# Sixteen operand tiles that each begin at another offset within 128 bytes

## The chip, the cores and the metric

The kernel runs on one core of a Trainium2 chip (trn2). The metric is the device time of one execution in microseconds (us). The core's engines are TensorE (PE in the profile; its weight loads, which run beside the matmuls, are PEld), VectorE (DVE), ScalarE (ACT), GpSimd (POOL) and SyncE (SP, here a queue for DMAs).

## The reference

One decoder block on x of 512 tokens x 1024 channels, float32. Two token mixers stand in parallel, a gated MLP in chunks (u, v_g) and a sparse attention whose keys an indexer selects (q, k, v, q_idx, k_idx). Their outputs are merged by sigmoid gates and projected; then comes a squared-ReLU MLP of 4096 channels.

```python
h = rmsnorm(x, norm1_g)
u, v_g, q, k, v, q_idx, k_idx, w_idx, gates = split_cols(h @ w_in, IN_SIZES)
y_a = sgu_mixer(gelu(u), gelu(v_g), w_s, b_s, sgu_ln_g, sgu_ln_b)
y_b = dsa_attention(rope(q), rope(k), v, rope(q_idx), rope(k_idx), w_idx)   # top 128 keys of a query
g = sigmoid(gates)                                                          # two gates
merged = g[0] * (y_a @ w_out_a) + g[1] * (y_b @ w_out_b)
x = x + merged @ w_o
h2 = rmsnorm(x, norm2_g)
x = x + square(relu(h2 @ w_ff_in)) @ w_ff_out
out = rmsnorm(x, norm_f_g)
```

## The kernel before

Activations are kept transposed, with channels on the 128 partitions and 512 tokens along them. A float32 product is made of three fp32r matmuls: each operand is split into a high part (ScalarE copies it to fp32r) and a low part (VectorE or POOL subtracts), and low x high, high x low and high x high are added in one PSUM bank. The input, scaled by the norm's weights, is 8 tiles `hTh[k]` (high) and 8 tiles `hTl[k]` (low) of 128 x 512, one pair for each 128 channels. After the attention the same 16 places hold `h2h[k]` and `h2l[k]`, the operand of the first MLP product.

`gemm` is the helper of most products. Its moving operand is the activation tile (512 columns), its stationary operand a 128 x 128 piece of a weight tile `wl` or `wh`; for each k it issues `wl[k]` with high (L146), `wh[k]` with low (L147) and `wh[k]` with high (L148). Each matmul has a weight load of its own. These products read the sixteen tiles as the moving operand:

- qi (index queries, 384 columns wide, 96 matmuls), k and q (96 each), ga and gb (the two gates, 192 each);
- f (the hidden layer of the MLP, `hidden`, 32 blocks of 24: 768).

Three more read them as the stationary operand, 128 tokens at a time: va at the start (values and the small index columns), and u and vg (`gmlp_in`, L409 to L411), where the weights `wh`, `wl` move.

Other products don't touch them: oa, ob (`yaT`, `ybs` moving), wo (`mT` moving), pp (`u` moving, `fp` stationary: the bulk of the second MLP product, in `products`), and the last part of that product (`f<-wh,fp`, L932 to L934: `wh`, `wl` moving, `fp` stationary).

The pools decide the addresses. In the built program every tile of `hTh`, `hTl`, `wh` and `wl` (pool G) begins at a multiple of 128 bytes in its partition. Pools E and F begin 96 bytes past a multiple of 128, and with them `mT`, `yaT`, `ybs`, `fp` and the tiles `u` that `products` uses. Pieces of a tile are 512 bytes or a multiple of it away from its beginning, so they stand at the same place within 128 bytes as the tile.

The order of the matmuls is that of a scheduler, which mixes neighbouring products; the generators `todo`, `fill` and `run` hand it the work.

Of the kernel before, what the change touches and what calls it, by code (L numbers as in the profile page):

```python
# [11 lines left out]
FR = mybir.dt.float32r  # L12
# [3 lines left out]
P = 128  # L16
S = 512
D = 1024
KD = D // P
# [14 lines left out]
def hybrid_block_kernel(ctx: ExitStack, tc: tile.TileContext, A: dict, out: bass.AP):  # L34
# [4 lines left out]
    G = ctx.enter_context(tc.tile_pool(name="G", bufs=1))  # L39
# [7 lines left out]
    def f32(ap):  # L47
        return ap.bitcast(F32)
# [125 lines left out]
        return get(0), get(1)  # L174


    hTh = [G.tile([P, S], FR, tag="hTh", bufs=KD, name=f"hTh{k}") for k in range(KD)]
    hTl = [G.tile([P, S], FR, tag="hTl", bufs=KD, name=f"hTl{k}") for k in range(KD)]
    VS = [E.tile([P, H, P], FR, tag="VS", bufs=NT, name=f"VS{j}") for j in range(NT)]
    R = E.tile([P, S], F32, name="R")  # L180
    rstd = G.tile([P, NT], F32, name="rstd")
# [43 lines left out]
    for t in raw2:  # L225
        t = f32(t.rearrange("p a b -> p (a b)"))
        raw += [t[:, i * NA:(i + 1) * NA] for i in range(3)]
    hl = []
    for k in range(KD):
# [5 lines left out]
        elif k < 6:  # L235
            t = E.tile([P, 13, P], FR, tag="pt", bufs=2, name=f"wa{k}").rearrange("p a b -> p (a b)")
# [486 lines left out]
    run(*[branch_b(m) for m in range(KD)])  # L723
    flush()

    h2h = [G.tile([P, S], FR, tag="hTh", bufs=KD, name=f"h2h{k}") for k in range(KD)]
    h2l = [G.tile([P, S], FR, tag="hTl", bufs=KD, name=f"h2l{k}") for k in range(KD)]
    x1T = []

    def proj_o(m):  # L730
# [357 lines left out]
```

## Time and profile before

| | us |
|---|---|
| median of 2 runs | 712.34 |
| lowest, highest | 711.14, 713.53 |
| profiled execution | 711.28 |
| its span, first to last instruction | 709.6 |
| TensorE busy in it | 693.9 |
| VectorE busy in it | 548.0 |

The length of a matmul in the profile runs from its start to its last result. The next one starts before that, so matmuls overlap in time, and the distance between two starts is what adds up.

### The profile page before, as it was taken

To read this page: it belongs to the slowest core of one execution; us is meant where nothing else is said; L and a number is where in the kernel's file an instruction comes from. 1 tells how busy PE (TensorE), PEld (TensorE's weight loads), DVE (VectorE), ACT (ScalarE), POOL (GpSimd) and SP (SyncE) were. 2 spreads that over 40 slices of the span, in tenths; PEclk is the share of its full clock that TensorE was granted. 3 is DMA by queue.
4 is the path that set the end of the run, shared out by engine and by line. 5 is a ranking of instruction groups with operands and counts; after the bars stand their busy time and mean duration, and the time that the engine had idled before them with its cause. 6 is when DMAs were issued, how large, how long until landed. Compare 5 with 4: busy or idle time off the path is not lost.

```text
span 709.6 us, 8958 instructions
## 1 busy us (share of the span) xinstructions
PE 693.9 (98%) x3232; PEld 575.1 (81%) x3232; DVE 548.0 (77%) x1015; ACT 329.7 (46%) x568; POOL 104.5 (15%) x61
## 2 busy tenths in 40 slices
PE   9999999899999899999999999999999999999996
PEld 8998888688887687778888888888888888888884
DVE  5588899976446857777442978979798997979995
ACT  5645633233244536564236765445352544535133
POOL 0053352444442242100000000000000000000001
PEclk9999999999999999999999999999999999999998
DMA  8735231234651454214443223142333214233023
GB/s 306 278 104 161 63 108 60 89 104 134 186 143 60 130 138 149 74 37 146 136 163 128 73 106 120 58 149 89 119 103 128 79 48 158 80 123 115 1 59 118
DMA packets 27356, 82.02 MB, mean 116 GB/s; under 512 B 4784, under 2 KB 6192, under 8 KB 25264
## 3 DMA queue, kind: packets, MB, share of 16 engines
q10 hardware_dynamic: 14688, 59.78, 26.0%
q1 hardware_dynamic: 12624, 21.67, 9.7%
q8 instruction: 25, 0.41, 0.2%
q14 instruction: 19, 0.16, 0.1%
HBM read 71.48 MB, written 2.10 MB: 104 GB/s over the span
## 4 chain that ended last, share of the span: by engine, by line
PE 59%; issue 0%; DVE 0%; ACT 0%; POOLq 0%; POOL 0%; ACTq 0%
PE f L148 8%; PE f L146 8%; PE f L147 8%; PE pp L882 6%; PE pp L884 6%; PE pp L883 6%; PE wo L146 2%; PE wo L147 2%; PE wo L148 2%; PE ob L146 1%; PE ob L147 1%; PE ob L148 1%; PE f L934 1%; PE f L933 1%; PE f L932 1%; PE pv L640 1%
## 5 line engine op out<-in xcount | busy, mean ns | idle before, releaser
L51 ACT ACTIVATE wh<-wr 128x1024 fp32r<-128x1024 f32 x88 | 92.9, 1057 | 127.2 <-PE f L148 40.4
L52 POOL TENSOR_TENSOR wl<-wr,wh 128x1024 fp32r<-128x1024 f32 x39 | 96.1, 2465 | 163.5 <-ACT wh L51 122.3
L146 PE MATMUL f<-h2h,wl 128*128 128x512 f32 x256 | 100.2, 391 | 0.0
L148 PE MATMUL f<-h2h,wh 128*128 128x512 f32 x256 | 100.0, 390 | 0.0
L147 PE MATMUL f<-h2l,wh 128*128 128x512 f32 x256 | 99.9, 390 | 0.0
L51 ACT ACTIVATE u<-w2r 128x512 fp32r<-128x512 f32 x98 | 59.1, 624 | 75.0 <-DVE w2r L810 25.4
L884 PE MATMUL pp<-u,fp 128*128 128x512 f32 x196 | 76.4, 390 | 0.0
L883 PE MATMUL pp<-u,fp 128*128 128x512 f32 x196 | 76.4, 390 | 0.0
L52 DVE TENSOR_TENSOR wl<-wr,wh 128x1024 fp32r<-128x1024 f32 x49 | 59.6, 1221 | 18.6 <-ACT wh L51 18.5
L882 PE MATMUL pp<-u,fp 128*128 128x512 f32 x196 | 72.1, 390 | 0.0
L895 DVE TENSOR_TENSOR P<-pp,P 128x512 f32<-128x512 f32 x84 | 54.4, 681 | 18.2 <-PE pp L884 18.0
L52 DVE TENSOR_TENSOR u<-w2r,u 128x512 fp32r<-128x512 f32 x98 | 64.4, 682 | 4.5 <-ACT u L51 4.5
L148 PEld LDWEIGHTS f<-h2h,wh 128*128 128x128 f32 x256 | 48.1, 188 | 10.1
L147 PEld LDWEIGHTS f<-h2l,wh 128*128 128x128 f32 x256 | 48.1, 188 | 10.0
L146 PEld LDWEIGHTS f<-h2h,wl 128*128 128x128 f32 x256 | 48.1, 188 | 9.9
L965 POOL TENSOR_TENSOR fss<-fss,mhalf 128x1 f32<-128x1 f32 x4 | 2.2, 547 | 317.7 <-DVE fss L964 317.7
L884 PEld LDWEIGHTS pp<-u,fp 128*128 128x128 f32 x196 | 36.8, 188 | 7.8
L882 PEld LDWEIGHTS pp<-u,fp 128*128 128x128 f32 x196 | 36.8, 188 | 7.8
L883 PEld LDWEIGHTS pp<-u,fp 128*128 128x128 f32 x196 | 36.8, 188 | 7.8
L51 ACT ACTIVATE fp<-fs 128x256 fp32r<-128x256 f32 (+1 forms) x28 | 17.6, 629 | 29.5 <-DVE fs L860 17.0
L838 DVE SCALAR_TENSOR_TENSOR fr<-f,R 128x512 f32<-128x512 f32 x32 | 21.8, 685 | 10.5 <-PE f L148 8.6
L146 PE MATMUL ga<-hTh,wl 128*128 128x512 f32 x64 | 25.1, 392 | 2.6 <-DVE mA L459 2.1
(251 smaller groups left out, 1563.5 us busy)
## 6 DMA issues: line engine op xcount, KB each, us to landing
wr<-in_f ACTq DMA_DIRECT2D x36, 512.0 KB, 3.5
w2r<-in_f2p ACTq DMA_DIRECT2D x14, 1024.0 KB, 4.9
wr<-in_wt ACTq DMA_DIRECT2D x26, 512.0 KB, 3.6
wr<-in_wuv ACTq DMA_DIRECT2D x8, 512.0 KB, 3.8
kq<-k_T SPq DMA_DIRECT2D x64, 64.0 KB, 2.2
wr<-in_wo ACTq DMA_DIRECT2D x8, 512.0 KB, 3.6
xT<-in_xT SPq DMA_DIRECT2D x8, 256.0 KB, 5.9
xn<-in_xn SPq DMA_DIRECT2D x2, 1024.0 KB, 9.1
```

Source lines behind the costliest of these rows:

```text
L51: ACT.activation(hi, src, AF.Copy)
L52: (eng or DVE).tensor_tensor(lo, src, f32(hi), op=ALU.subtract)
L146: PE.matmul(dst, wl[:, k], bh, start=(k == 0), stop=False)
L147: PE.matmul(dst, wh[:, k], bl, start=False, stop=False)
L148: PE.matmul(dst, wh[:, k], bh, start=False, stop=(k == K - 1))
L640: PE.matmul(b[:, s0 * P:], VS[j][:, h], rhs, start=(n == 0 and j == 0), stop=(n == 1 and j == NT - 1))
L838: DVE.scalar_tensor_tensor(r, b, 0.0, R2, op0=ALU.max, op1=ALU.mult)
L882: PE.matmul(b[j], fl, u[:, 0], start=(q == 0), stop=False)
L883: PE.matmul(b[j], fh, u[:, 1], start=False, stop=False)
L884: PE.matmul(b[j], fh, u[:, 0], start=False, stop=(q == 1))
L895: DVE.tensor_tensor(sums[name, j], b[j], sums[name, j], op=ALU.add)
L932: PE.matmul(b[j], fl[:, t], wh[:, k], start=(q == 0 and k == 0), stop=False)
```

## The change

Each of the sixteen tiles gets 32 more columns (128 bytes), and the 512 columns that are used begin at a column from a table: 0 to 30, another one for each tile. That is 0 to 120 bytes past the tile's beginning, which stays at a multiple of 128 bytes. The second use of the places, `h2h` and `h2l`, takes the same table. Nothing else is edited: the sequence of instructions on each of the five engines is the same in both built programs. The other tiles move up by 2048 bytes.

```diff
-    hTh = [G.tile([P, S], FR, tag="hTh", bufs=KD, name=f"hTh{k}") for k in range(KD)]
-    hTl = [G.tile([P, S], FR, tag="hTl", bufs=KD, name=f"hTl{k}") for k in range(KD)]
+
+    AT = dict(hTh=(0, 1, 2, 4, 8, 12, 16, 24), hTl=(26, 30, 3, 6, 10, 14, 20, 28))
+
+    def operand(tag, k, name):
+        t = G.tile([P, S + 32], FR, tag=tag, bufs=KD, name=f"{name}{k}")
+        return t[:, AT[tag][k]:AT[tag][k] + S]
+
+    hTh = [operand("hTh", k, "hTh") for k in range(KD)]
+    hTl = [operand("hTl", k, "hTl") for k in range(KD)]
...
-    h2h = [G.tile([P, S], FR, tag="hTh", bufs=KD, name=f"h2h{k}") for k in range(KD)]
-    h2l = [G.tile([P, S], FR, tag="hTl", bufs=KD, name=f"h2l{k}") for k in range(KD)]
+    h2h = [operand("hTh", k, "h2h") for k in range(KD)]
+    h2l = [operand("hTl", k, "h2l") for k in range(KD)]
```

## Rows read from the trace of the kernel before

**Rows 1.** The page: its head, TensorE's busy time with its share of the span and its instructions, and the clock granted to TensorE in 40 equal slices of the span (tenths, 9 is 90% or more).

```profile
span 709.6 us, 8958 instructions
...
PE 693.9 (98%) x3232; PEld 575.1 (81%) x3232; DVE 548.0 (77%) x1015; ACT 329.7 (46%) x568; POOL 104.5 (15%) x61
...
PEclk9999999999999999999999999999999999999998
```

**Rows 2.** Groups of TensorE's matmuls by line, tiles and shape: out<-in, count | busy us, mean ns of one | idle us before them.

```profile
L146 PE MATMUL f<-h2h,wl 128*128 128x512 f32 x256 | 100.2, 391 | 0.0
L148 PE MATMUL f<-h2h,wh 128*128 128x512 f32 x256 | 100.0, 390 | 0.0
L147 PE MATMUL f<-h2l,wh 128*128 128x512 f32 x256 | 99.9, 390 | 0.0
L884 PE MATMUL pp<-u,fp 128*128 128x512 f32 x196 | 76.4, 390 | 0.0
...
L147 PE MATMUL gb<-hTl,wh 128*128 128x512 f32 x64 | 25.3, 395 | 0.0
L147 PE MATMUL wo<-mT,wh 128*128 128x512 f32 x64 | 25.1, 396 | 0.0
...
L148 PE MATMUL ga<-hTh,wh 128*128 128x512 f32 x64 | 24.9, 389 | 0.0
...
L148 PE MATMUL oa<-yaTh,wh 128*128 128x512 f32 x32 | 12.7, 396 | 0.0
...
L934 PE MATMUL f<-wh,fp 128*128 128x512 f32 x32 | 12.6, 395 | 0.0
...
L148 PE MATMUL ob<-ybsh,wh 128*128 128x512 f32 x32 | 12.5, 395 | 0.0
...
L410 PE MATMUL u<-wl,hTh 128*128 128x512 f32 x32 | 12.4, 389 | 0.0
```

**Rows 3.** The timeline of TensorE in the middle of the f matmuls: start us, length us, engine, line. The first and the last of eleven matmuls that follow each other, and a weight load after the second of them (426 us).

```profile
425.75 0.39 PE L148 MATMUL f<-h2h,wh 128*128 128x512 f32 x1
425.97 0.39 PE L146 MATMUL f<-h2h,wl 128*128 128x512 f32 x1
...
428.01 0.39 PE L146 MATMUL f<-h2h,wl 128*128 128x512 f32 x1
...
425.98 0.19 PEld L147 LDWEIGHTS f<-h2l,wh 128*128 128x128 f32 x1
```

**Rows 4.** The same in the middle of the wo matmuls, the first and the last of eleven that follow each other.

```profile
339.82 0.40 PE L148 MATMUL wo<-mT,wh 128*128 128x512 f32 x1
...
342.15 0.40 PE L146 MATMUL wo<-mT,wl 128*128 128x512 f32 x1
```

**Rows 5.** Stretches of the span (us from its start): their length, then for PE, PEld, DVE, ACT and POOL the busy us (and instructions), the granted clock, the DMA share and GB/s. In this order: the f matmuls, the wo matmuls, and the gates ga beside VectorE's top-k work.

```profile
424.00:444.00 20.00, 20.00 (x90) 16.55 (x89) 16.35 (x27) 11.44 (x20) 0.00 (x0) 1.00 0.43 141
330.00:360.00 30.00, 30.00 (x130) 24.16 (x129) 15.48 (x18) 10.05 (x12) 0.00 (x0) 1.00 0.41 126
...
122.00:134.00 12.00, 9.36 (x41) 7.14 (x40) 12.00 (x23) 3.26 (x5) 4.94 (x2) 1.00 0.26 87
```

**Rows 6.** The timeline of TensorE among the qi matmuls, 384 columns wide: the first and the last of eleven that follow each other.

```profile
37.12 0.33 PE L147 MATMUL qi<-hTl,wh 128*128 128x384 f32 x1
...
38.85 0.33 PE L148 MATMUL qi<-hTh,wh 128*128 128x384 f32 x1
```

**Rows 7.** Instructions that read hTl, by product: count, then shortest/median/longest length in ns, start of the first and of the last in us, shape. The last row is from the same view of hTh.

```profile
L147 PE MATMUL ga<-hTl,wh x64: 389/389/398, 102.8 to 148.8; 128*128 128x512 f32 x64
...
L147 PE MATMUL gb<-hTl,wh x64: 387/389/478, 198.6 to 295.0; 128*128 128x512 f32 x64
...
L147 PE MATMUL qi<-hTl,wh x32: 334/334/346, 31.4 to 50.0; 128*128 128x384 f32 x32
...
L409 PE MATMUL vg<-wh,hTl x32: 387/396/397, 50.3 to 80.1; 128*128 128x512 f32 x32
...
L147 PE MATMUL k<-hTl,wh x32: 387/389/398, 149.5 to 228.1; 128*128 128x512 f32 x32
...
L147 PE MATMUL q<-hTl,wh x32: 389/389/477, 163.2 to 247.7; 128*128 128x512 f32 x32
...
L410 PE MATMUL vg<-wl,hTh x32: 389/393/398, 50.5 to 80.4; 128*128 128x512 f32 x32
```

**Rows 8.** The timeline of TensorE from 110 to 140 us, the two matmuls before which it sat idle: [idle us <-what ended it].

```profile
125.06 0.50 PE L146 MATMUL ga<-hTh,wl 128*128 128x512 f32 x1 [0.56 <-POOL wl L52]
...
132.87 0.47 PE L146 MATMUL ga<-hTh,wl 128*128 128x512 f32 x1 [2.08 <-DVE mA L459]
```

**Rows 9.** Operations of VectorE and ScalarE that write the sixteen tiles, as groups by shape (columns as in rows 2).

```profile
L739 DVE SCALAR_TENSOR_TENSOR h2l<-x1T,g,h2h 128x512 fp32r<-128x512 f32 x8 | 6.0, 747 | 1.6 <-ACT h2h L738 1.6
...
L284 ACT ACTIVATE hTh<-xT,g 128x512 fp32r<-128x512 f32 x8 | 5.7, 718 | 3.4 <-DMA xT<-in_xT 1.9 <-DMA g<-in_g 1.4
...
L738 ACT ACTIVATE h2h<-x1T,g 128x512 fp32r<-128x512 f32 x8 | 5.7, 714 | 6.6 <-DVE x1T L737 6.6
...
L286 DVE SCALAR_TENSOR_TENSOR hTl<-xT,g,hTh 128x512 fp32r<-128x512 f32 x7 | 5.3, 751 | 6.2 <-ACT hTh L284 6.2
```

**Rows 10.** The eight warm-up matmuls at the start: count, shortest/median/longest length in ns.

```profile
L281 PE MATMUL va<-wah x8: 628/628/793, 1.5 to 4.7; 128*128 128x512 f32 x8
```

## Prediction

> **What bounds the kernel now.** I read the page's busy shares first: TensorE is busy 693.9 of 709.6 us, at the full clock in nearly every slice [rows 1]. The next engine, VectorE, is at 77%. So the question is how long one matmul takes, and second where TensorE waits and could swallow a loss.
>
> The groups by shape give the length of one matmul [rows 2]. All of those I use are 128x512 fp32r, each with a weight load of its own, and still they fall into two families. The hidden products f, the gates ga, the u projection and the products pp have 389 to 391 ns. oa, wo, ob and the last products (`f<-wh,fp`) have 395 to 396 ns. Lengths overlap, because matmuls are pipelined; what counts is the distance between two starts. Among the f matmuls ten distances are 428.01 - 425.75 = 2.26 us, 226 ns each [rows 3]; among wo 342.15 - 339.82 = 2.33 us, 233 ns each [rows 4]. So the difference of the lengths, 6 to 7 ns, is also the difference in pace, at the same shape and the same clock of 1.00 in both windows [rows 5].
>
> What sets the families apart? I lay the built program's addresses beside the rows. Each time the weight load of the next matmul runs inside the current one (a load starts at 425.98 for 0.19 us, just after the matmul of 425.97) [rows 3]. Compare where the moving operand of the running matmul starts, within 128 bytes, with where the weights being loaded start. f, ga, u: both at 0. pp: both at 96. oa, wo, ob: moving 96, weights 0. Last products: moving 0, weights 96. Equal starts go with 389 to 391, unequal with 395 to 396, whichever of the two stands at 96. That pool E against pool G would explain it as well is a rival below.
>
> How much of a matmul is such meeting? The 384 wide qi matmuls, also with equal starts, follow each other at (38.85 - 37.12)/10 = 173 ns [rows 6]. From 384 to 512 columns the pace grows by 53 to 54 ns, 0.42 ns a column; 512 columns alone would be 212 to 216 ns, so the 227 hold 11 to 15 ns beyond columns, and the 233 hold 17 to 21. I take this excess as the price of the two reads meeting; that is an inference from the rows, not something that they show.
>
> **The change, part by part.** No instruction is added, removed or moved: the sequences of all five engines are the same in both built programs, so there is no new wait and no queue is moved past. SBUF grows by 16 x 128 = 2048 bytes a partition and the rest of the tiles move by multiples of 128, so oa, wo, ob, pp and the last products keep their pair of starts: 0. What changes is the start of hTh, hTl, h2h, h2l: 4 times the table's number, 0 to 120 bytes past a multiple of 128.
>
> Of the 24 matmuls of one projection (8 steps of k; high twice, low once) only the two with tile 0 of the high part keep equal starts: 22 of 24 become unequal. Price of one that becomes unequal: the step between the families, 6.5 ns (396 - 389.5). It is one step for one distance (96 bytes, or 32 the other way), and fifteen other distances are coming; the rows bound it from 0 (a distance that meets as little as equal starts) to 9 ns (the longest ga matmul that is not waiting, 398 against 389 [rows 7]). I take 6.5, since both unequal groups of the trace agree on it. Term by term:
>
> - Hidden products f: 768 x 22/24 = 704 at 6.5 ns = 4.6 us. They run with TensorE full and VectorE at 16.35 of 20 us [rows 5], so all of it is on the path.
> - Gates ga and the u projection: from 81 to about 130 us TensorE is ahead of VectorE. It waits 0.56 and 2.08 us there, for POOL and for VectorE's ga evacuation behind its top-k work [rows 8], and VectorE is full (12.00 of 12 us) while TensorE has 9.36 [rows 5]. u (88 x 6.5 = 0.6 us) and the ga before 132.9 us (some 110 x 6.5 = 0.7 us) fit into this 2.6 us: 0. Without that cover they would cost 1.3 us. The ga after it, from 133 to 149 us at 227 ns some 72, of which 66 unequal: 0.4 us.
> - gb, k, q: 384 matmuls, 352 unequal. They are mixed with attention work; the medians are still 389 [rows 7], the means 395 for gb [rows 2]. Part of the price is already paid by such neighbours, part falls into softmax waits: 5 ns, 1.8 us.
> - vg: medians 396 and 393 already [rows 7]: 88 at 1 ns, 0.1 us. qi, 384 wide, median 334: 88 at 4 ns, 0.35 us.
> - va at the start (192 matmuls, hT as weights): its moving operands mostly start at 96 against 0 now, so one unequal distance is replaced by another: 0, with 1.2 us either way as bound.
> - ScalarE and VectorE write and read these tiles in 32 operations of 714 to 751 ns [rows 9]; an element per lane and step is what they do at any start that the trace shows, and they are spread over stages where TensorE is full: 0.
>
> Sum: 4.6 + 0.4 + 1.8 + 0.1 + 0.35 = 7.2 us. The profiled execution took 711.28 us (span 709.6); 711.3 + 7.2 = 718.5. The median of the runs, 712.34, lies 1.06 above that execution: **719.5 us**, 1.0% slower. With 2 ns in place of 6.5 it is 714.5, with 9 ns 722.3: the forecast's own range is 714.5 to 722.5.
>
> **The rivals.**
>
> *No change.* The two families could be due to the pool (E against G: far apart in SBUF) or to who wrote the tile, not to the start within 128 bytes; the rows cannot separate these, as every E tile starts at 96. pp speaks against it a little: both its operands are in the late pool and it has 390 [rows 2], so it isn't the pool alone, but a pair of pools would still do. Or small distances count like 0. Then 712 us, 709.5 to 714.5.
> [...]
>
> *Slower by more than 2%: reads that straddle.* Every moving operand of the trace starts at a multiple of 32 bytes. Now 10 of 24 matmuls (k = 1, 2 of the high tiles, six of the low tiles) start off a multiple of 16, and 3 of 24 off a multiple of 8. If such a read fetches two pieces for each piece before, these alone get slower. At half pace, 227 ns more (the only rows with a much slower 128x512 are the eight warm-up matmuls at the very start, 628 against 389 ns long [rows 10]), 3 of 24 of 1344 matmuls are 168 x 0.227 = 38 us: 758 us; 10 of 24 would be 127 us. It decides from 14.2 - 7.2 = 7 us over 560 matmuls, 13 ns each; there the time is 727. For it: no row excludes it. Against it: 512 neighbouring elements need not be fetched anew for each.
> [...]
>
> *Faster.* Equal starts may be the bad meeting, and 96 a worse one, while other distances avoid it. If all of the excess of 12 ns went for the 704 + 66 + 352 + 88 = 1210 matmuls on the path, 14.5 us go: 698 us. A third of that, the likelier size since the distances are mixed: 707. Against it: the two distances known are both worse than 0, and 387 is the shortest length in the gb and k rows, 2 ns under their median [rows 7].
>
> **How the numbers follow.** Forecast 0.52, no change 0.24, straddling reads 0.14, faster 0.10. The likeliest gives 719.5. From 709 to 730: below lie some 0.07 of the faster case, above some 0.12 of straddling, so 0.81 is inside. 2% (about what a measurement of this kernel can tell from no change) is 14.2 us: 698.1 and 726.6. Faster by over 2%: 0.03, which takes all of the excess; slower: the straddling rival and a tail of the forecast with over 12 ns a matmul, 0.17; within: 0.80.
>
> **What the profile after would show.** Right: f goes from 390 to about 396 ns and u from 389 to 396, while pp (390), oa and wo (396) stay, and the counts, the waits and the clock stay. The mean may split by line: the two lines with hTh against the one with hTl. Wrong: f at 390 (pool, not start); f bimodal with some far above 400 (straddling), to be seen in the largest of the length of `f<-h2l,wh` against the other two lines; f below 387 (faster). If f has its 396 and the time hasn't grown, the path is elsewhere than I think. If pp or wo move as well, the start isn't what acts but the place in SBUF.

## Result and profile after

The changed kernel takes 720.09 us (median of 2 runs, 719.27 to 720.90) against 712.34: ratio 1.0105, 95% interval 1.0072 to 1.0137. That is slower by more than the runs scatter and by less than 2%. The profiled execution took 719.27 us.

The head of the page after answers to [rows 1]: the same instructions and the same clock, and TensorE is busy 7.1 us longer in a span that is 7.9 us longer.

```profile
span 717.5 us, 8958 instructions
...
PE 701.0 (98%) x3232; PEld 576.4 (80%) x3232; DVE 551.8 (77%) x1015; ACT 330.3 (46%) x568; POOL 104.1 (15%) x61
...
PEclk9999999999999999999999999999999999999998
```

The groups of TensorE after (count | busy us, mean ns | idle us before) answer to [rows 2].

```profile
L148 PE MATMUL f<-h2h,wh 128*128 128x512 f32 x256 | 101.5, 397 | 0.0
L146 PE MATMUL f<-h2h,wl 128*128 128x512 f32 x256 | 101.3, 396 | 0.0
L147 PE MATMUL f<-h2l,wh 128*128 128x512 f32 x256 | 101.0, 394 | 0.0
L891 PE MATMUL pp<-u,fp 128*128 128x512 f32 x196 | 76.4, 390 | 0.0
...
L147 PE MATMUL gb<-hTl,wh 128*128 128x512 f32 x64 | 25.5, 398 | 0.0
L148 PE MATMUL ga<-hTh,wh 128*128 128x512 f32 x64 | 25.4, 397 | 0.0
L147 PE MATMUL wo<-mT,wh 128*128 128x512 f32 x64 | 25.1, 395 | 0.0
...
L148 PE MATMUL oa<-yaTh,wh 128*128 128x512 f32 x32 | 12.7, 396 | 0.0
...
L417 PE MATMUL u<-wl,hTh 128*128 128x512 f32 x32 | 12.6, 395 | 0.0
```

f, u and ga have joined the longer family; pp, wo and oa stand where they were. The pace went with the length: in the timeline after, twelve distances between f matmuls are 433.41 - 430.62 = 2.79 us, 232.5 ns each, against 226 in [rows 3].

```profile
430.62 0.40 PE L148 MATMUL f<-h2h,wh 128*128 128x512 f32 x1
...
433.41 0.40 PE L148 MATMUL f<-h2h,wh 128*128 128x512 f32 x1
```

Where the time went is read from the start of each product's first matmul, before and after: from row to row the lag grows. The view by tile (count, shortest/median/longest ns, first to last start) answers to [rows 7]; the third row is from the same view of h2l, whose row before ran from 367.6 to 679.5 us.

```profile
L147 PE MATMUL ga<-hTl,wh x64: 388/395/403, 103.9 to 150.3; 128*128 128x512 f32 x64
L147 PE MATMUL gb<-hTl,wh x64: 387/394/477, 200.5 to 299.2; 128*128 128x512 f32 x64
...
L147 PE MATMUL f<-h2l,wh x256: 388/395/480, 371.8 to 687.5; 128*128 128x512 f32 x128
```

ga begins 103.9 - 102.8 = 1.1 us later, gb 1.9, the last gb 4.2, f 4.2, the last f 8.0. So 3.8 us are lost inside f, about half of the whole, 2.3 while gb runs among the attention's matmuls, and 1.1 before ga.

### The profile page after: what moved, and what is told of

Read it like the earlier page. It is cut to its first block, busy times and chain, and to the rows that moved or that the text cites. A ratio compares the mean times of both kernels' runs of the same rounds, so it can differ in the third digit from the quotient of the medians.

```text
span 717.5 us, 8958 instructions
## 1 busy us (share of the span) xinstructions
PE 701.0 (98%) x3232; PEld 576.4 (80%) x3232; DVE 551.8 (77%) x1015; ACT 330.3 (46%) x568; POOL 104.1 (15%) x61
## 4 chain that ended last, share of the span: by engine, by line
PE 59%; issue 0%; DVE 0%; ACT 0%; POOLq 0%; POOL 0%; ACTq 0%
PE f L148 8%; PE f L146 8%; PE f L147 8%; PE pp L891 6%; PE pp L890 6%; PE pp L889 6%; PE wo L146 2%; PE wo L147 2%; PE wo L148 2%; PE ob L146 1%; PE ob L147 1%; PE ob L148 1%; PE f L941 1%; PE f L939 1%; PE f L940 1%; PE pv L647 1%
## 5 line engine op out<-in xcount | busy, mean ns | idle before, releaser
L148 PE MATMUL f<-h2h,wh 128*128 128x512 f32 x256 | 101.5, 397 | 0.0
L148 PEld LDWEIGHTS f<-h2h,wh 128*128 128x128 f32 x256 | 48.1, 188 | 11.1
```

The lines of the kernel that those rows point to most:

```text
L148: PE.matmul(dst, wh[:, k], bh, start=False, stop=(k == K - 1))
```

## The experiments

The theory on record: what counts is where, within 128 bytes, the moving operand of a matmul starts against where the weights start that are loaded beside it. Rivals: the place in SBUF; the pool (E against G); that neighbouring matmuls differ in their distance (the "mixture" below); reads that straddle, from starts off 16 bytes. "Distance" below is the start of the moving operand less that of the weights. The runs of the kernel before beside these had medians of 711.6 to 711.9 us (712.8, one run, beside the scan by 4 bytes and the last experiment).

**Longer tiles alone.** The changed kernel with all offsets zero.

```diff
-    AT = dict(hTh=(0, 1, 2, 4, 8, 12, 16, 24), hTl=(26, 30, 3, 6, 10, 14, 20, 28))
+    AT = dict(hTh=(0,) * KD, hTl=(0,) * KD)
```

> The sixteen tiles are 128 bytes longer as in the change, all begin at column 0. Theory (the distance within 128 bytes between the start of the moving operand and of the weights that load beside it): all distances are 0 again, so f<-h2h,wh has a mean of 390 ns, as before (397 with the change), and the time is that of the kernel before, 712 us, ratio 1.000. Rival (the place in SBUF: tiles moved by up to 2048 bytes): f at 396, ratio 1.010.

Measured: 717.62 us, 1.0074 (1.0056 to 1.0092). Its groups:

```profile
L147 PE MATMUL f<-h2l,wh 128*128 128x512 f32 x256 | 101.0, 395 | 0.0
L148 PE MATMUL f<-h2h,wh 128*128 128x512 f32 x256 | 101.0, 394 | 0.0
L146 PE MATMUL f<-h2h,wl 128*128 128x512 f32 x256 | 100.9, 394 | 0.0
```

Every tile starts at the same place within 128 bytes as before, and still f has 394 to 395: the theory modulo 128 falls. A tile is now 2176 bytes long, 8.5 times 256, so every second one starts 128 away modulo 256. The theory put on record next was modulo 512 (a tile is 4.25 times that); the scan by 16 bytes below makes 256 of it. The rival of this run, the place in SBUF as such, forecast 396 and isn't refuted by it; the control below does that.

**All offsets 96 bytes.** `AT` is 24 for every tile.

> All sixteen tiles begin at column 24, 96 bytes past a multiple of 128, so the distance to the weights is one and the same in all of f, ga, gb, k, q. Theory: the distance of 96 that oa and wo have, so f and ga get their 396 ns; f 768 x 6.5 ns = 5.0, ga after VectorE's wait 0.5, gb, k, q 1.9, the rest 0.5, together 7.9 us: 720, ratio 1.011. Rival pool (oa and wo are slow as their moving operand is in the late pool, not for its start): f stays at 390, ratio 1.000. Rival mixture (it costs that neighbouring matmuls differ in their distance, not the distance itself): f stays at 390, ratio 1.000.

Measured: 719.02 us, 1.0092 (1.0073 to 1.0111), f at 395 to 398. As the theory said, but this doesn't support it: the long tiles, which the run above found guilty, are in here too.

**Pools E and F moved by 32 bytes** in the kernel before, so that the moving operands of oa, wo and ob, and the weights of the last products, start at distance 0 from their partners. The sixteen tiles are left alone.

```diff
+    G.tile([P, 8], F32, name="pad")
```

> The kernel before, with 32 bytes of padding at the end of the first pool, so that the pools E and F begin at a multiple of 128 too and every operand of the kernel has distance 0. Theory: oa, ob, wo and the last products (480 matmuls) go from 396 to 390 ns, 480 x 6.5 = 3.1 us: 709.2, ratio 0.9956. Rival pool: they stay at 396, ratio 1.000.

Measured: 709.11 us, 0.9947 (0.9932 to 0.9963).

```profile
L147 PE MATMUL wo<-mT,wh 128*128 128x512 f32 x64 | 24.7, 389 | 0.0
...
L148 PE MATMUL oa<-yaTh,wh 128*128 128x512 f32 x32 | 12.4, 389 | 0.0
...
L932 PE MATMUL f<-wh,fp 128*128 128x512 f32 x32 | 12.4, 389 | 0.0
```

All three groups fell from 395 or 396 to 389. They stay in their pools, so the pool as a cause falls. This one line makes the fastest kernel of the study, ahead of both the kernel before and the one after. Its gain is larger than the medians say: in its profile the granted clock was 0.80 from 130 to 136 us (1.00 before), and k's first matmul starts 2.2 us later than before; yet the span is 2.0 us shorter, so some 4 us are gained behind that.

**The same pools moved by 160 bytes**: distance 0 modulo 128, but 128 modulo 256.

```diff
+    G.tile([P, 40], F32, name="pad")
```

> As e3, but with 160 bytes of padding: the later pools begin at a multiple of 128 which is 256 past a multiple of 512, where the first pool's tiles are 128 past one. Theory (modulo 512): oa and wo stay at 394 to 396 ns, ratio 0.999 to 1.001. Rival (modulo 128): 390 as in e3, ratio 0.995.

Measured: 711.48 us, 1.000 (0.9989 to 1.0011).

```profile
L147 PE MATMUL wo<-mT,wh 128*128 128x512 f32 x64 | 25.1, 395 | 0.0
...
L148 PE MATMUL oa<-yaTh,wh 128*128 128x512 f32 x32 | 12.6, 395 | 0.0
```

With 32 bytes of padding 389, with 160 again 395. Between these two runs nothing differs but the 128 bytes: modulo 128 is refuted without the long tiles (256 and 512 both stand).

**Offsets without longer tiles.** Each eight tiles become pieces of one tile, laid in the order of their offsets so that none overlaps; first with all offsets zero as a control, then with the table.

```diff
+    def operands(tag, name):
+        t = G.tile([P, KD * S + 128], FR, tag=tag, bufs=1, name=name)
+        out = [None] * KD
+        for p, k in enumerate(sorted(range(KD), key=lambda k: AT[tag][k])):
+            out[k] = t[:, p * S + AT[tag][k]:(p + 1) * S + AT[tag][k]]
+        return out
...
```

> The eight high tiles are pieces of one tile of 8 x 2048 + 512 bytes, the eight low ones of another, each piece at a multiple of 2048 from the beginning: every start is 128 past a multiple of 512, as in the kernel before, and all other tiles keep their place within 512 bytes. No instruction moves. Theory now (the distance modulo 512 bytes between the start of the moving operand and that of the weights loaded beside it; a distance of 0 gives 227 ns from start to start, others 229 to 236): f at 390 ns, 712 us, ratio 1.000. Rival (the place in SBUF as such: the other tiles stand 1024 bytes higher): f above 393, 715 or more.

> The same, with the table's offsets of the change (0 to 120 bytes) in pieces that otherwise begin at 128 past a multiple of 512: the offsets without the longer tiles. Theory (distance modulo 512): nearly all distances are unequal to 0, f at 395 to 397 ns, 718 to 720 us, ratio 1.009 to 1.011; the offsets and the longer tiles cost much the same each, and not their sum together. Rival (the longer tiles alone do it, and offsets under 128 add the third that is missing, 717.6 to 720.1): f at 391 to 392, 714 to 715.

Measured: the control 713.20 us, 1.0015 (1.0006 to 1.0024), f at 390 to 391; with the table 716.86 us, 1.0076 (1.0061 to 1.0091), under the 718 to 720 expected, f at 394 to 395. In the control f has its length of before, though the other tiles stand 1024 bytes higher: the place in SBUF falls. The 2.1 us by which its profile's span is longer don't come from distances. k's first matmul already starts 2.1 us later than before, and f's last 2.2; 1.6 of it came while ga ran, behind TensorE's wait of 2.1 us for VectorE. There the granted clock (the value before the DMA share; the control, then before) was 0.71 on the mean of 5 us, against 1.00 before:

```profile
135.00:140.00 5.00, 5.00 (x17) 4.02 (x16) 5.00 (x16) 1.58 (x2) 2.88 (x2) 0.71 0.31 75
135.00:140.00 5.00, 5.00 (x23) 4.13 (x22) 5.00 (x15) 1.58 (x2) 2.87 (x2) 1.00 0.36 105
```

So the offsets alone cost about as much as the longer tiles alone, and both together (1.0105) less than the sum: f has 394 to 395 ns with either and 394 to 397 with both, so a matmul that was off already didn't get off twice.

**Which distances.** Only the weights of the f matmuls are moved here, 16t bytes further in block t (24 matmuls, t from 0 to 31), with the high and the low half in one tile; h2h and h2l stay. In the next run, the same with 4t bytes.

```diff
-            h = G.tile([P, 1024], FR, tag="wh", bufs=3, name=f"wh{n}")
-            l = G.tile([P, 1024], FR, tag="wl", bufs=3, name=f"wl{n}")
+            w = G.tile([P, 2 * 1024 + 128], FR, tag="wh", bufs=3, name=f"w{n}")
+            o = at_w.get(n, 0)
+            h, l = w[:, o:o + 1024], w[:, o + 1024:o + 2048]
...
+    at_w.update({len(wsrc) + m: 4 * m for m in range(4 * NG)})
...
```

> The kernel before, with high and low weights of a step in one tile; the 32 blocks of f have their weights begin 16 t bytes further, block t = 0 to 31, all else as before. One distance for all of a block. Theory (modulo 512): block 0 at 227 ns from start to start, the others at 229 to 236, blocks 8, 16 and 24 (128, 256, 384) among them, mean about 232. Rival (modulo 128): blocks 8, 16 and 24 at 227 like block 0. Rival mixture (what costs is that the distance changes between neighbouring matmuls): all blocks at 227.

Measured: 714.60 us (one run). The starts of the first matmuls of blocks 15, 16 and 17, and of 23, 24 and 25:

```profile
512.55 0.40 PE L148 MATMUL f<-h2h,w 128*128 128x512 f32 x1
...
518.01 0.39 PE L148 MATMUL f<-h2h,w 128*128 128x512 f32 x1
...
523.45 0.39 PE L148 MATMUL f<-h2h,w 128*128 128x512 f32 x1
...
595.07 0.39 PE L148 MATMUL f<-h2h,w 128*128 128x512 f32 x1
...
600.67 0.40 PE L148 MATMUL f<-h2h,w 128*128 128x512 f32 x1
...
606.27 0.39 PE L148 MATMUL f<-h2h,w 128*128 128x512 f32 x1
```

Block 16 (weights 256 bytes further) takes 523.45 - 518.01 = 5.44 us, 226.7 ns a matmul: as if not moved. Block 24 (384 further, 128 modulo 256) takes 5.60, 233.3 ns. The expectation (modulo 512) missed with block 16, and the mixture falls with block 24, whose matmuls all have one distance. Over the run, blocks t and t + 16 have nearly the same pace, leaving out the first three and their partners, as other matmuls come between the first: in this scan of 0 to 496 bytes the pace repeats after 256. At distances 0 and 16 it is about 227, at 64 and 80 229 to 230, at the rest 232 to 234. Block 17, at distance 240, kept 227, but block 1, at the same distance, did so only at its start:

```profile
374.97 0.39 PE L148 MATMUL f<-h2h,w 128*128 128x512 f32 x1
...
376.10 0.40 PE L150 MATMUL f<-h2h,w 128*128 128x512 f32 x1
...
379.94 0.40 PE L150 MATMUL f<-h2h,w 128*128 128x512 f32 x1
...
382.04 0.40 PE L150 MATMUL f<-h2h,w 128*128 128x512 f32 x1
```

The first five distances between starts make 1.13 us, 226 ns each; then transposes (`xn`) come between, and the last nine make 2.10 us, 233 ns each. So at one distance this run has both paces, and what ran before them differs.

> As e7, but in steps of 4 bytes: the weights of block t of f begin 4 t bytes further, t = 0 to 31, so distances of 0 to -124 bytes, three of four off a multiple of 16. Theory (the distance modulo 256 bytes, as e7 showed it: 0, 16 and 240 at 227 ns from start to start, 64 and 80 at 229 to 230, the others at 232 to 234): blocks 0 and 4 (distance 0 and 240) at 227, blocks off a multiple of 16 between 226 and 236 like those on one. Rival straddling (a read that starts off 16 or 8 bytes takes longer): blocks off 16 bytes stand above all of e7's, over 236, the odd ones most.

Measured: 715.37 us (one run). The first and the last matmul of blocks 21 (84 bytes) and 25 (100 bytes), 23 distances each:

```profile
565.42 0.39 PE L148 MATMUL f<-h2h,w 128*128 128x512 f32 x1
...
570.82 0.39 PE L150 MATMUL f<-h2h,w 128*128 128x512 f32 x1
...
607.01 0.39 PE L148 MATMUL f<-h2h,w 128*128 128x512 f32 x1
...
612.30 0.39 PE L150 MATMUL f<-h2h,w 128*128 128x512 f32 x1
```

Block 21 is the slowest, 5.40/23 = 235 ns; block 25 has 5.29/23 = 230. Weights that start off 16, 8 or 4 bytes lie between 227 and 235, where the multiples of 16 lie too. So no load that starts off 16 bytes stands above the 236 that the rival asked for; the straddling rival of the prediction was about the moving operand, and there the kernel after decides: `f<-h2l`, with six of eight steps off a multiple of 16, has 394 ns, the least of the three f lines. So the straddling rival falls. The expectation of 227 at distance 240 missed again (block 4: 233), while block 30, at 136, has 227.

**A scan that told little.** As the scan by 4, but with each half in a tile of its own, longer by 128 bytes.

> The kernel before, where the weight tiles of the 32 blocks of the hidden products begin at another column each: block t at column t, so at 4 t bytes, high and low alike. Within a block all 24 matmuls have one distance, -4 t bytes. Theory: the distance between two starts of f differs by block, 227 ns for block 0, about 233 for block 24 (weights at 96, moving at 0, as in the last products), the others between 224 and 238; the mean over the blocks near the 233 of f in the changed kernel. Rival mixture: each block at 227, since nothing changes within a block. Rival straddling: the 24 blocks whose column is no multiple of 4 stand apart from the 8 others, above all the odd columns.

Measured: 718.16 us (one run), f at 395 on all three lines. The longer tiles move every second buffer by 128 bytes, so that in each block either the high or the low weights are 128 bytes off the distance they were given: inconclusive, and the reason for the one-tile form above.

**Which of the two weights.** Only the low half of the f weights is 128 bytes further.

```diff
+            h, l = w[:, :1024], w[:, o + 1024:o + 2048]
...
+    at_w.update({len(wsrc) + m: 32 for m in range(4 * NG)})
...
```

> The kernel before, with the low weights wl of f alone 128 bytes further (modulo 256 the distance that costs 233 ns in e7), the high ones as before. In a step of k come wl with high (L148 here), wh with low (L149), wh with high (L150), so the matmul with wl in the array runs beside the load of wh, and the last of the three beside the load of wl. Theory (the load that runs beside the matmul counts): L150 lengthens, L148 and L149 stay at 227 ns or little above. Rival (the weights already loaded for the matmul itself): L148 lengthens, L150 stays.

Measured: 714.42 us (one run). The three lines of a step (L148: low half in the array, high loading; L149: high and high; L150: high in the array, low loading):

```profile
L148 PE MATMUL f<-h2h,w 128*128 128x512 f32 x256 | 101.9, 398 | 0.0
L150 PE MATMUL f<-h2h,w 128*128 128x512 f32 x256 | 101.4, 396 | 0.0
L149 PE MATMUL f<-h2l,w 128*128 128x512 f32 x256 | 100.0, 391 | 0.0
```

Both lines that touch the low half lengthen, the third doesn't: neither answer alone. Whether it is the weights being loaded, those loaded before, or both, stays open.

## Why the prediction was right, step by step

**The price per matmul: equal against unequal starts holds, the period doesn't.** That equal starts go with 390 ns and unequal with 396 is confirmed by an intervention on each side: the one line of padding took wo from 396 to 389 ([rows 2, 4]), and moving f's weights alone took f from 390 to between 394 and 396. The step that failed is "Compare where the moving operand of the running matmul starts, within 128 bytes": in the runs it is within 256 bytes (wo at 389 ns with 32 bytes of padding, 395 with 160; 226.7 ns in block 16 of the scan, 256 bytes further). So is "the rest of the tiles move by multiples of 128": by that sentence a move of 128 bytes does nothing, while block 24 of the scan, moved by 384, has 233.3 ns against 226.7, and the longer tiles alone, which move every second one of the sixteen by 128, cost 0.74%. That the number came out in spite of it is luck of two kinds. The distances fell the same way, because the sixteen tiles together grow by 2048 bytes, 8 times 256, so the other tiles kept their distances anyway, and because, with the longer tiles too, only tile 0 of the high part keeps the distance 0. And terms that were too large were made up by a wait that no step had (gb, k, q below).

**Hidden products f: 4.6 predicted, 3.8 measured.** 3.8 us over the 704 unequal matmuls is 5.4 ns each in place of 6.5; the mean lengths rose by 7, 5 and 4 ns on the three lines. The single value 6.5 was too coarse: the scans have 227 to 235 ns of pace, by distance.

**Gates and u: 0.4 predicted, about 0.9 measured.** u was to be free, since TensorE waits for VectorE later. But u's first matmul starts 0.56 us later and ga's 1.1: 0.55 was lost there and never regained. The wait ahead of ga is not a fixed slack. After, the wait for POOL of [rows 8] is gone and that for VectorE is 1.97 in place of 2.08, and it ends 1.0 us later:

```profile
133.90 0.47 PE L146 MATMUL ga<-hTh,wl 128*128 128x512 f32 x1 [1.97 <-DVE mA L466]
```

VectorE is full in that stretch [rows 5] and began its top-k late itself. Its row by line had 80.4 to 147.4 us before; after:

```profile
L516 DVE MAX8 m<-sc x48: 398/539/695, 80.9 to 148.4; 128x8 f32<-128x512 f32 x16, 128x8 f32<-128x384 f32 x16, 128x8 f32<-128x256 f32 x16
```

I read this from the starts alone: it works on scores that TensorE makes earlier, among matmuls that the change lengthens as well. The slack counts from VectorE's own start, and that moved by 0.5 to 1.0 us. The ga matmuls between 104 and 133 us were covered as predicted: the lag is 1.1 us at their start and 1.0 at 133.90. From there to the first k matmul it grows by some 0.4, the term for the late ga.

**gb, k, q: 1.8 predicted, 2.7 measured.** The medians rose from 389 to 394 or 395 and the means by 3 ns; 384 at 3 ns is 1.2, less than the 1.8: the 5 ns were too many. The rest is a wait that no step of the prediction had. Before, VectorE's addition and POOL's subtraction began within 0.01 us of each other; VectorE took 0.68 us and POOL 2.96:

```profile
229.92 2.96 POOL L52 TENSOR_TENSOR wl<-wr,wh 128x1024 fp32r<-128x1024 f32 x1 [5.07 <-ACT wh L51]
229.93 0.68 DVE L328 TENSOR_TENSOR k_a<-k_a,k_b 128x512 f32<-128x512 f32 x1
```

After, the same two: POOL 2.38, and the addition 2.91. The softmax behind it reaches TensorE late.

```profile
231.98 2.38 POOL L52 TENSOR_TENSOR wl<-wr,wh 128x1024 fp32r<-128x1024 f32 x1 [5.06 <-ACT wh L51]
232.00 2.91 DVE L335 TENSOR_TENSOR k_a<-k_a,k_b 128x512 f32<-128x512 f32 x1
...
235.68 0.44 PE L635 MATMUL pt<-ident,p 128*128 128x128 f32 x2 [2.02 <-DVE yp L654]
```

Each time one of the two is the long one; that the other holds it up is my reading. In the other eleven of the twelve profiles here it is POOL, with 2.95 to 2.97 us against 0.68; in all twelve POOL's start is recorded first, by 0.02 us or less, so what decides isn't shown. In the 45 us around it, 2 us later after than before, TensorE's busy time (second column) is 42.48 before

```profile
215.00:260.00 45.00, 42.48 (x212) 34.34 (x212) 33.52 (x76) 21.86 (x48) 12.54 (x5) 1.00 0.37 102
```

and 40.81 after, so 1.7 us more are idle:

```profile
217.00:262.00 45.00, 40.81 (x204) 32.91 (x203) 34.45 (x75) 22.29 (x48) 10.47 (x5) 1.00 0.35 99
```

The profile with the table's offsets but no longer tiles gives the size, since there the longest such addition is 1.68 us and TensorE doesn't wait for yp. Up to the meeting the two run together: a q matmul that starts at 230.77 us before starts at 232.73 there and at 232.81 after. Behind it, a gb matmul before, with the offsets alone, and after:

```profile
248.38 0.47 PE L146 MATMUL gb<-hTh,wl 128*128 128x512 f32 x1
250.38 0.48 PE L146 MATMUL gb<-hTh,wl 128*128 128x512 f32 x1
252.22 0.48 PE L146 MATMUL gb<-hTh,wl 128*128 128x512 f32 x1
```

That is 2.0 us later with the offsets alone and 3.8 after: the wait made 1.8 us of the 2.7. (The two programs differ in the tiles' length too, and no run sets the meeting alone.) Without it the profiled execution would be about 6 us longer than before, in place of 7.9.

**The small terms.** va was predicted at 0 and lost 0.3 (qi starts so much later); in the control, whose distances are those of before, qi starts 0.4 later too, so this is no price of the change. qi cost 0.1 instead of 0.35, vg 0.15 instead of 0.1. The operations of [rows 9] have means of 714 to 752 ns after, each within 1 ns of before: 0, as predicted. Together the terms are 7.95 us against 7.2.

**The rivals.** No change falls: the pool is refuted by the 32 bytes of padding. Straddling falls by `f<-h2l` after (394 ns) and, for the weights, by the scan by 4 bytes. Faster falls: no block of the two scans was under 226.7 ns, so no distance in them was better than 0.

## What to carry to other kernels

In this kernel, with TensorE full of 512 wide fp32r matmuls that each load weights, the short groups (389 to 391 ns) had the moving operands and the weights at the same place modulo 256 bytes. In a kernel like it that is worth a try: read the places from the built program's addresses. Here moving two pools by 32 bytes took wo and oa from 395 or 396 ns to 389 and the time to 0.9947. A tile that is lengthened to hold an offset moves its neighbours too, so test the length without the offset (here it alone cost 0.74%). A wait of an engine that is off the path is slack only if the engine that it waits for doesn't start later itself: TensorE's wait for VectorE before ga was 1.97 us in place of 2.08, but it ended 1.0 us later.

## What the runs showed of the hardware

Two things were not expected: that the pace came back after 256 bytes (226.7 ns in block 16 of the scan, 256 further, and 233.3 in block 24, 384 further), which is the only period of 128, 256 and 512 that agrees with all runs here, and that at one distance it differs with what ran before (233 ns at the end of block 1 and 227 in block 17). The kernel before shows the second at distance 0 as well: behind a stretch of pp, the first seven distances of f make 424.84 - 423.23 = 1.61 us, 230 ns each, before they settle at 227; with the pools moved by 32 bytes, so that the change from pp to f meets at distance 0 too, the same seven make 424.59 - 423.01 = 1.58 us, 226 ns each. What meets in these 256 bytes isn't shown by any row; that weight reads and moving reads collide stays an inference from the starts.
